# A two-layer hybrid decoder trunk: weight pairs in pieces of 512 columns, retention loads moved ahead, and a norm written over its input

## The chip, the cores and the metric

The kernel runs on one core of a Trainium2 chip. The metric is the device time of one execution in microseconds (us). The engines are named as the profile names them: PE (TensorE, matmul) and PEld (its weight loads), DVE (VectorE), ACT (ScalarE), POOL (GpSimd) and SP (SyncE). POOL and SP only issue DMAs here, apart from a few small copies on POOL.

## What is computed

The reference is one inference step of a two-layer trunk with d_model 1024, on 256 prompt positions and 8 sequences of 8 new positions, 320 columns together. Cut to what matters:

```python
for l in range(2):
    x = x + 0.5 * swiglu_ffn(rmsnorm(x, ffn1_norm[l]), ffn1_w_gu[l], ffn1_w_down[l])
    h = rmsnorm(x, mix_norm[l])
    q, k, v, g_ret, u, z, xbc, dt, gates = split(h @ w_in[l])
    y_ret = retention_branch(q, k, v, g_ret, state_ret[l])   # 4 heads, decay masks, gated norm
    y_s5  = s5_branch(u, state_s5[l])                        # 64 groups, complex diagonal scan
    y_ssd = ssd_branch(z, xbc, dt, state_ssm[l], state_conv[l])
    x = x + (sum of sigmoid(gate_i) * y_i) @ w_out[l]
    x = x + 0.5 * swiglu_ffn(rmsnorm(x, ffn2_norm[l]), ffn2_w_gu[l], ffn2_w_down[l])
y = rmsnorm(x, final_norm)
```

Outputs are y and the new states of the three branches.

## The kernel before, in words

Activations lie transposed: a tile `t` of 128 channels by 320 columns, eight of them for d_model. They come from one pool of 53 buffers (`NT`).

**Weights.** All matrices are float32 in memory. `stream` (L267) yields blocks of 128x128 in the order of use. It loads a chunk of 1024 columns (`CH`, eight blocks) with a DMA on SP's queue into one of three raw buffers (`wraw`), and turns it into a float32r pair: ACT copies it to `whi` (L280), DVE subtracts that from the raw chunk to make `wlo` (L281). There are two buffers each of `whi` and `wlo`. `proj` (L287) multiplies each block with three matmuls: high by high (L294), high by low (L295), low by high (L296), 24 matmuls a chunk, 554 chunks in all. `split` (L299) makes the same kind of pair of an activation: ACT L304, DVE L305.

**Order.** The program is built with a tile framework. Each engine's instructions are put in one fixed order when the kernel is built, by a priority that follows the order of the source, and by when a buffer of their pool is free. An instruction written inside `high_priority(offset=n)` counts as n instructions earlier; the load and the two copies of a chunk have n = 120 (`AHEAD`), and evacuations of some projections have 600 (`SOON`). On the chip an engine runs its list in order, each instruction waiting for its semaphores.

**Stages of a layer.** The first feed-forward net (in layer 0 the tables of the S5 branch are built beside it, L1178), then the mixer, then the second net. In the mixer, `norm` (L372) makes h: for each of eight tiles DVE computes h = X * gain * r into a new tile (L377) and `split` makes the pair. Until that is ready, the first projections (`ssd_dt` L429, `s5_u` L1194, `conv` L502) use pairs of the unnormalised X. X is read from DRAM again near the layer's end (L1427).

`weave` (L381) runs a list of main units, mostly projections, and advances side generators evenly beside it: SSD groups (L588), S5 blocks (L1209), and in the last two weaves of the mixer (L1397, L1398) the four retention heads (`ret_head`, L864), two a weave one after the other. A head has twelve steps. In its first it issues, on POOL's queue, two loads of its state (L870) and two table loads (L871): its decay mask `mk` (`tab(2 + hd)`) and the decay table `qd` (`tab(6)`, the same for all heads). `tab` (L206) takes a tile `t` and issues a DMA (L208). After two empty steps come the scores, multiplied by the mask (L882 to L884), and the decayed queries (L886); the pair of the keys (`stack`, L568: ACT L573, DVE L574) spread to the array's rows (L583); the outputs; the state update and its stores (L931, L940); then the loads of two gate rows `sd` (L943, `fetch` L1319), the norm over the head (`rstd_of`, L330: DVE L338 to L347, PE L335 and L350), and the gating (L953, L954). `ret_qk` (L793) makes queries and keys; DVE evacuates it at L808. `s5_block` loads an S5 state (L1226) that DVE reads at L1257.

Of the kernel before, what the change touches and what calls it, by code (L numbers as in the profile page):

```python
# [9 lines left out]
F32 = mybir.dt.float32  # L10
F32R = mybir.dt.float32r
I32 = mybir.dt.int32
AF = mybir.ActivationFunctionType
ALU = mybir.AluOpType
# [19 lines left out]
CH = 1024  # L34
# [14 lines left out]
S5P = ((0,), (1, 2), (3, 4), (5, 6), (7,))  # L49
AHEAD = 120  # L50
# [102 lines left out]
    return t.rearrange(f"p ({' '.join(names)}) -> p {' '.join(names)}", **dict(zip(names, shape)))  # L153


class Trunk:
    def __init__(self, tc, ap, depth, es):
        self.tc, self.nc, self.ap, self.depth = tc, tc.nc, ap, depth
        self.uid = 0
        P = lambda n, b, **kw: es.enter_context(tc.tile_pool(name=n, bufs=b, **kw))  # L160
        self.cp = P("consts", 1)
        self.wr = P("wraw", 3)
        self.wh = P("whi", 2)
        self.wl = P("wlo", 2)
        self.tp = P("t", NT)
        self.pA = P("a", NA)
        self.pB = P("b", 4)
        self.pS = P("s", 7)
        self.pC = P("c", 4)
        self.sm = P("sm", 1)  # L170
        self.pp = P("pp", 4, space=PSUM)
        self.pb = P("pb", 4, space=PSUM)
        self.dr = P("dr", 1, space=DRAM)
# [93 lines left out]
    def stream(self, name, l, width=128):  # L267
        nc = self.nc
        src = self.ap[name][l]
        n = src.shape[1]  # L270

        def gen():
            for c in range(0, n, CH):
                w = min(CH, n - c)
                raw = self.s("wraw", [128, CH], pool=self.wr)
                hi = self.s("whi", [128, CH], F32R, pool=self.wh)
                lo = self.s("wlo", [128, CH], F32R, pool=self.wl)
                with self.tc.high_priority(offset=AHEAD):
                    nc.sync.dma_start(out=raw[:, :w], in_=src[:, c:c + w])
                    nc.scalar.activation(hi[:, :w], raw[:, :w], AF.Copy)  # L280
                    nc.vector.tensor_tensor(lo[:, :w], raw[:, :w], hi[:, :w].bitcast(F32), op=ALU.subtract)  # L281
                for b in range(0, w, width):
                    yield hi[:, b:b + width], lo[:, b:b + width]

        return gen()

# [9 lines left out]
            nc.tensor.matmul(p[:, :T], wl, xh, start=False, stop=k == n - 1)  # L296
        return p

    def split(self, src, hi=None):  # L299

        nc = self.nc
        hi = self.t(F32R)
        lo = self.t(F32R)
        nc.scalar.activation(hi, src, AF.Copy)  # L304
        nc.vector.tensor_tensor(lo, src, hi.bitcast(F32), op=ALU.subtract)  # L305
        return hi, lo
# [65 lines left out]
    def norm(self, l, name, r):  # L372
        nc = self.nc
        hs = []
        for k in range(KD):
            h = self.t()
            nc.vector.scalar_tensor_tensor(h, self.X[k], self.col(l, name, k), r, op0=ALU.mult, op1=ALU.mult)  # L377
            hs.append(self.split(h))
        return hs

# [409 lines left out]
    def ret_tabs(self):  # L790
        self.rot = self.tab(0), self.tab(1)

    def ret_qk(self, l, h, rot):  # L793

        nc = self.nc
        sts = {}

        def unit(nme, hd):
            if nme not in sts:
                sts[nme] = self.stream(f"w_{nme}", l)  # L800
            cos, sin = self.rot
            p = self.proj(sts[nme], h())
            sw = self.t()
            o = self.t()
            with self.soon():
                nc.scalar.activation(sw[0:64], p[64:128, :T], AF.Copy)
                nc.scalar.activation(sw[64:128], p[0:64, :T], AF.Copy)
                nc.vector.tensor_tensor(o, p[:, :T], cos, op=ALU.mult)  # L808
            nc.vector.tensor_tensor(sw, sw, sin, op=ALU.mult)
            nc.vector.tensor_tensor(o, o, sw, op=ALU.add)  # L810
            rot[nme, hd] = o

        return [lambda n=n, hd=hd: unit(n, hd) for n in "qk" for hd in range(RH)]
# [50 lines left out]
    def ret_head(self, l, hd, rot, v, vs, sd, out):  # L864
        nc, C, ap = self.nc, self.C, self.ap
# [2 lines left out]
        s0 = [self.A(4, 256) for _ in range(2)]  # L868
        for i in range(2):
            nc.gpsimd.dma_start(out=s0[i], in_=ap["ret_in"][l][:, hd, 4 * i:4 * i + 4])  # L870
        mk, qd = self.tab(2 + hd), self.tab(6)  # L871
        yield
        yield
        q, k = rot["q", hd], rot["k", hd]
        vv, VS = v[hd // 2], vs[hd // 2]
        c8 = float(np.exp(LS * np.log1p(-np.exp2(-5.0 - hd))))
# [34 lines left out]
        for e in range(2):  # L911
            vc = slice(hd % 2 * 256 + e * 128, hd % 2 * 256 + e * 128 + 128)
            po = self.ps()
            nc.tensor.matmul(po[:, 0:256], vv[:, 0, vc], sc[:, 0:256], start=True, stop=False)
            nc.tensor.matmul(po[:, 128:256], vv[:, 1, vc], sc[:, 256:384], start=False, stop=True)
            nc.tensor.matmul(po[:, 256:320], vv[:, 2, vc], sc[:, 384:], start=True, stop=False)
            for hf in range(2):
                nc.tensor.matmul(po[:, 256 + 32 * hf:288 + 32 * hf], ys[hf][:, e * 128:e * 128 + 128], C["pick"],
                                 start=False, stop=hf == 1)
            o = self.t()  # L920
            S.activation(o, po[:, :T], AF.Copy)
            os.append(o)
            yield

        vh = slice(hd % 2 * 256, hd % 2 * 256 + 256)
        pp = self.ps()
# [13 lines left out]
                nc.gpsimd.dma_start(out=ap["ret_s"][l][:, hd, 4 * (b2 // 2):4 * (b2 // 2) + 4], in_=s0[b2 // 2])  # L940
                yield

        sgs = [self.fetch(sd[:, 2 * hd + e]) for e in range(2)]  # L943
        pm = self.ps()
        for e in range(2):
            nc.tensor.matmul(pm[:, :T], self.ones[256], os[e], start=e == 0, stop=e == 1)
# [3 lines left out]
        r = self.rstd(os, 256)  # L950
# [377 lines left out]
    def layer(self, l):  # L1328
        nc, ap = self.nc, self.ap
# [8 lines left out]
        hs, r = self.scaled(l, "mix_norm")  # L1338
# [3 lines left out]
        h = lambda: H[0]  # L1342
# [18 lines left out]
        s5 = lambda *bs: [(self.s5_block(l, Q, ud, yd, b), self.S5_STEPS) for b in bs]  # L1361
        zu = lambda g: self.ssd_gate(l, h, g, xg[g][2:], S["z"], yg[g])
# [3 lines left out]
        rot, v, vs, heads = {}, [], [], {}  # L1366
# [3 lines left out]
        sd = self.dr.tile([128, KD, T], F32, name=self.nm("sd"))  # L1370
# [6 lines left out]
        rg = self.ret_gate(l, h, S["g"], sd)  # L1377
        take = lambda n: [free.pop(0) for _ in range(n)]
# [4 lines left out]
        x, o = xu(3), ou(1)  # L1383
        self.weave(take(W4) + x[:2] + zu(1) + blend(x[2:], take(W5)) + take(W6) + o[:4] + [self.ret_tabs] + o[4:], ssd(2), s5(*S5P[0]))
        self.weave(take(W7) + qk[:2] + zu(2) + qk[2:5] + take(W8) + blend(qk[5:], ou(2)), ssd(3), s5(*S5P[1]))
        o = ou(3)
        self.weave(vu[0] + zu(3) + [vr] + vu[1] + o[:2] + [vr] + o[2:], s5(*S5P[2]))
        yret = []
        ret = [(self.ret_head(l, hd, rot, v, vs, sd, yret), self.RET_STEPS) for hd in range(RH)]

        def gate2(m):
            gt = self.gate(S["t2"], h())
            V.scalar_tensor_tensor(merged[m], gt, 1.0, merged[m], op0=ALU.add, op1=ALU.mult)

        g2 = [lambda m=m: gate2(m) for m in range(KD)]
        n = len(free)
        self.weave(rg[:4] + g2[:4] + take(n // 2), ret[:2], s5(*S5P[3]))  # L1397
        self.weave(rg[4:] + g2[4:] + take(len(free)), ret[2:], s5(*S5P[4]))  # L1398
        so = self.stream("ret_w_o", l)
        ys5 = []  # L1400
# [183 lines left out]
```

## Time and profile before

| what | value |
|---|---|
| median of 3 runs | 2372.28 us (2371.87 to 2375.01) |
| the profiled execution's own time | 2377.88 us |
| its span, first to last instruction | 2376.1 us |
| instructions | 41534 |
| HBM traffic | 455.63 MB, mean 192 GB/s |

The span is what one execution shows between its first and its last instruction; the few microseconds around it make the execution's time. Busy time of PE is modelled, since its matmuls overlap: a PE that is shown busy may still run below its peak. An idle time is put down to the instruction that released the waiting one.

### The profile page before, as it was taken

The page shows a single profiled execution, that of the slowest core. Times are in us where ns is not written, and L with a number is a line of the kernel's source. Part 1 is how long each engine was busy: PE and PEld are TensorE (multiplying, and loading weights), DVE is VectorE, ACT ScalarE, POOL GpSimd, SP SyncE. Part 2 cuts the span into 40 slices and gives each one's busy share as a digit, 9 for nine tenths or more (in the row PEclk, how much of TensorE's full clock was granted, in tenths as well). Part 3 has the DMA queues.
Part 4 walks back from the last instruction along what each step waited for, and adds up shares of the span by engine and source line. Part 5 has one row for each costly group of instructions (what it writes and reads, how often), then busy time and mean ns, then how long its engine had stood idle before and what let it go on. Part 6 is the DMA issues. An engine that isn't in the chain of part 4 may idle for free.

```text
span 2376.1 us, 41534 instructions
## 1 busy us (share of the span) xinstructions
PE 2294.7 (97%) x15798; PEld 2177.9 (92%) x15798; DVE 1754.0 (74%) x3398; ACT 1231.0 (52%) x2261; POOL 439.5 (18%) x858
## 2 busy tenths in 40 slices
PE   7999999999999999999999999999999999999998
PEld 7999989988898889999999999899888887999998
DVE  7989788798776556767876687888887665666554
ACT  4444477676454444444443445876574544544332
POOL 0111242221223230001000013432211232200000
PEclk9999999999999999999999999999999999999999
DMA  5767656756666565455556665766756674755553
GB/s 172 229 209 223 209 173 225 242 189 206 225 200 218 188 204 169 150 164 177 179 173 192 180 210 167 245 196 212 232 161 212 212 257 140 226 150 146 149 150 110
DMA packets 130856, 455.63 MB, mean 192 GB/s; under 512 B 19744, under 2 KB 23552, under 8 KB 130656
## 3 DMA queue, kind: packets, MB, share of 16 engines
q1 hardware_dynamic: 82080, 293.11, 40.7%
q0 software_dynamic: 48576, 159.86, 19.9%
q8 instruction: 124, 2.03, 0.3%
q14 instruction: 76, 0.62, 0.1%
HBM read 381.31 MB, written 72.89 MB: 191 GB/s over the span
## 4 chain that ended last, share of the span: by engine, by line
PE 78%; ACT 6%; DVE 6%; issue 5%; DMA 2%; POOL 2%; SPq 0%; DVEq 0%; POOLq 0%; ACTq 0%
PE pp L294 22%; PE pp L296 22%; PE pp L295 22%; DVE wlo L281 2%; ACT whi L280 2%; DMA t<-in_tabs 2%; PE pb L1238 1%; ACT B L671 1%; PE pb L350 1%; PE pb L711 1%; PE pb L718 1%; PE pb L687 1%; PE pp L836 1%; PE pp L837 1%; PE pp L838 0%
## 5 line engine op out<-in xcount | busy, mean ns | idle before, releaser
L294 PE MATMUL pp<-t,whi 128*128 128x320 f32 x4304 | 1344.2, 313 | 30.6 <-ACT t L365 12.3
L296 PE MATMUL pp<-t,wlo 128*128 128x320 f32 x4304 | 1339.5, 312 | 11.3 <-DVE wlo L281 11.1
L295 PE MATMUL pp<-t,whi 128*128 128x320 f32 x4304 | 1339.4, 312 | 0.4 <-DVE t L366 0.4
L280 ACT ACTIVATE whi<-wraw 128x1024 fp32r<-128x1024 f32 x554 | 586.2, 1059 | 779.1 <-issue 388.7
L281 DVE TENSOR_TENSOR wlo<-wraw,whi 128x1024 fp32r<-128x1024 f32 x554 | 676.7, 1222 | 265.5 <-ACT whi L280 261.9
L294 PEld LDWEIGHTS pp<-t,whi 128*128 128x128 f32 x4304 | 811.0, 189 | 49.1 <-ACT t L365 12.3
L296 PEld LDWEIGHTS pp<-t,wlo 128*128 128x128 f32 x4304 | 811.7, 189 | 25.4 <-DVE wlo L281 18.0
L295 PEld LDWEIGHTS pp<-t,whi 128*128 128x128 f32 x4304 | 812.3, 189 | 8.0 <-issue 2.6
L304 ACT ACTIVATE t<-t 128x320 fp32r<-128x320 f32 x184 | 84.3, 463 | 61.8 <-DVE t L1421 28.7
L305 DVE TENSOR_TENSOR t<-t,t 128x320 fp32r<-128x320 f32 x184 | 88.4, 486 | 18.1 <-ACT t L304 16.9
L526 DVE SCALAR_TENSOR_TENSOR acc<-xpad,cols,acc 128x344 f32<-128x344 f32 x144 | 80.0, 571 | 4.3 <-ACT acc L523 3.6
L405 DVE TENSOR_TENSOR t<-pp,t 128x320 f32<-128x320 f32 x88 | 42.7, 486 | 45.0 <-PE pp L296 39.0
L411 DVE TENSOR_TENSOR t<-t,pp 128x320 f32<-128x320 f32 x88 | 42.6, 484 | 38.6 <-PE pp L296 37.7
L671 ACT ACTIVATE B<-C,tk 128x128 f32<-128x128 f32 x192 | 63.0, 392 | 0.1
L325 ACT ACTIVATE t<-t 128x320 f32<-128x320 f32 x104 | 47.2, 460 | 25.7 <-DVE t L416 12.2
L416 DVE SCALAR_TENSOR_TENSOR t<-pp,t 128x320 f32<-128x320 f32 x64 | 31.2, 488 | 35.1 <-PE pp L296 35.0
L406 ACT ACTIVATE t<-t 128x320 f32<-128x320 f32 x88 | 40.4, 459 | 22.1 <-DVE t L405 22.0
L519 POOL COPY cso<-xpad 128x3 f32<-128x3 f32 x48 | 29.1, 607 | 104.9 <-ACT xpad L514 79.0
L1148 POOL DMA_DIRECT2D kd<-t x64 | 32.6, 516 | 78.5 <-issue 73.4
L407 DVE TENSOR_TENSOR t<-t,t 128x320 f32<-128x320 f32 x88 | 42.7, 485 | 4.5 <-ACT t L406 4.5
L1166 POOL DMA_DIRECT2D pk<-A x16 | 8.8, 552 | 188.4 <-DVE A L1164 188.4
L709 DVE TENSOR_TENSOR A<-A,dec 128x512 f32<-128x512 f32 x64 | 42.3, 685 | 1.3 <-PE pb L699 1.3
(368 smaller groups left out, 2508.8 us busy)
## 6 DMA issues: line engine op xcount, KB each, us to landing
wraw<-in_w_gu SPq DMA_DIRECT2D x176, 512.0 KB, 3.5
wraw<-in_w_down SPq DMA_DIRECT2D x88, 512.0 KB, 3.6
wraw<-in_w_xbc SPq DMA_DIRECT2D x48, 512.0 KB, 4.3
wraw<-in_w_gate SPq DMA_DIRECT2D x48, 512.0 KB, 4.6
A<-in_ssm_in POOLq DMA_DIRECT2D x32, 512.0 KB, 6.0
out_ssm_s<-A POOLq DMA_DIRECT2D x32, 512.0 KB, 5.1
wraw<-in_w_z SPq DMA_DIRECT2D x32, 512.0 KB, 4.8
wraw<-in_ssd_w_o SPq DMA_DIRECT2D x32, 512.0 KB, 3.7
```

The lines of the kernel that those rows point to most:

```text
L280: nc.scalar.activation(hi[:, :w], raw[:, :w], AF.Copy)
L281: nc.vector.tensor_tensor(lo[:, :w], raw[:, :w], hi[:, :w].bitcast(F32), op=ALU.subtract)
L294: nc.tensor.matmul(p[:, :T], wh, xh, start=k == 0, stop=False)
L295: nc.tensor.matmul(p[:, :T], wh, xl, start=False, stop=False)
L296: nc.tensor.matmul(p[:, :T], wl, xh, start=False, stop=k == n - 1)
L304: nc.scalar.activation(hi, src, AF.Copy)
L305: nc.vector.tensor_tensor(lo, src, hi.bitcast(F32), op=ALU.subtract)
L325: self.nc.scalar.activation(q, x, AF.Square)
L405: V.tensor_tensor(hid[i], p[:, :T], r, op=ALU.mult)
L407: V.tensor_tensor(hid[i], hid[i], r, op=ALU.mult)
L526: nc.vector.scalar_tensor_tensor(acc[:, :n], xp[:, r:r + n], self.col(l, "conv_w", 4 * i + r), acc[:, :n], op0=ALU.mult, op1=ALU.add)
L671: S.activation(lm[:, e, o:o + 128], bc[:, i0:i0 + 128], AF.Relu, scale=-1.0, bias=tk[:, b, c:c + 1])
```

## The change

It does four things. Weight chunks are still loaded in 1024 columns to three raw buffers, but the pairs are made in pieces of 512 columns (`CW`), with four buffers each of `whi` and `wlo` in place of two, each of half the size. `norm` writes h over X instead of into a new tile. A unit `ret_masks` loads the masks of heads 0 and 1 and the decay table in the last weave before retention, and those of heads 2 and 3 at the end of the first retention weave; `ret_head` no longer loads them. The two gate rows of a head are fetched before its state update instead of after it. (An argument of `split` that nothing used is dropped.)

```diff
+CW = 512
...
-        self.wh = P("whi", 2)
-        self.wl = P("wlo", 2)
+        self.wh = P("whi", 4)
+        self.wl = P("wlo", 4)
...
                 raw = self.s("wraw", [128, CH], pool=self.wr)
-                hi = self.s("whi", [128, CH], F32R, pool=self.wh)
-                lo = self.s("wlo", [128, CH], F32R, pool=self.wl)
                 with self.tc.high_priority(offset=AHEAD):
                     nc.sync.dma_start(out=raw[:, :w], in_=src[:, c:c + w])
-                    nc.scalar.activation(hi[:, :w], raw[:, :w], AF.Copy)
-                    nc.vector.tensor_tensor(lo[:, :w], raw[:, :w], hi[:, :w].bitcast(F32), op=ALU.subtract)
-                for b in range(0, w, width):
-                    yield hi[:, b:b + width], lo[:, b:b + width]
+                for o in range(0, w, CW):
+                    m = min(CW, w - o)
+                    hi = self.s("whi", [128, CW], F32R, pool=self.wh)
+                    lo = self.s("wlo", [128, CW], F32R, pool=self.wl)
+                    with self.tc.high_priority(offset=AHEAD):
+                        nc.scalar.activation(hi[:, :m], raw[:, o:o + m], AF.Copy)
+                        nc.vector.tensor_tensor(lo[:, :m], raw[:, o:o + m], hi[:, :m].bitcast(F32), op=ALU.subtract)
+                    for b in range(0, m, width):
+                        yield hi[:, b:b + width], lo[:, b:b + width]
...
         for k in range(KD):
-            h = self.t()
-            nc.vector.scalar_tensor_tensor(h, self.X[k], self.col(l, name, k), r, op0=ALU.mult, op1=ALU.mult)
+            h = self.X[k]
+            nc.vector.scalar_tensor_tensor(h, h, self.col(l, name, k), r, op0=ALU.mult, op1=ALU.mult)
             hs.append(self.split(h))
...
+    def ret_masks(self, *heads):
+
+        def unit():
+            if 0 in heads:
+                self.qd, self.mks = self.tab(6), {}
+            for hd in heads:
+                self.mks[hd] = self.tab(2 + hd)
+        return [unit]
...
-        mk, qd = self.tab(2 + hd), self.tab(6)
-        yield
-        yield
+        yield
+        yield
+        mk, qd = self.mks[hd], self.qd
...
             os.append(o)
             yield
+        sgs = [self.fetch(sd[:, 2 * hd + e]) for e in range(2)]
...
-        sgs = [self.fetch(sd[:, 2 * hd + e]) for e in range(2)]
         pm = self.ps()
...
-        self.weave(vu[0] + zu(3) + [vr] + vu[1] + o[:2] + [vr] + o[2:], s5(*S5P[2]))
+        self.weave(vu[0] + zu(3) + [vr] + vu[1] + o[:2] + [vr] + o[2:4] + self.ret_masks(0, 1) + o[4:], s5(*S5P[2]))
...
-        self.weave(rg[:4] + g2[:4] + take(n // 2), ret[:2], s5(*S5P[3]))
+        self.weave(rg[:4] + g2[:4] + take(n // 2) + self.ret_masks(2, 3), ret[:2], s5(*S5P[3]))
```

## Rows read from the trace of the kernel before

**Rows 1.** The page's part 1: busy us (share of the span) xinstructions.

```profile
PE 2294.7 (97%) x15798; PEld 2177.9 (92%) x15798; DVE 1754.0 (74%) x3398; ACT 1231.0 (52%) x2261; POOL 439.5 (18%) x858
```

**Rows 2.** Stretches of 25 us: busy time of each engine, PEclk, DMA share, GB/s.

```profile
50.00:75.00 25.00, 24.78 (x169) 24.51 (x168) 24.66 (x63) 14.61 (x28) 2.69 (x5) 1.00 0.59 183
...
1725.00:1750.00 25.00, 24.42 (x176) 23.65 (x175) 23.42 (x47) 22.25 (x53) 0.00 (x0) 1.00 0.45 141
...
2150.00:2175.00 25.00, 25.00 (x173) 25.00 (x172) 15.18 (x22) 9.93 (x14) 0.00 (x0) 1.00 0.51 148
```

**Rows 3.** Waits of PE: us in total, times, longest us.

```profile
PE pp L296 <- DVE wlo L281: 11.1, 16, 1.9
PE pb L583 <- DVE S L574: 9.3, 8, 2.0
PE pb L350 <- DVE rs L347: 8.5, 7, 2.3
...
PE pp L294 <- DVE t L808: 5.9, 2, 3.0
PE pp L294 <- ACT whi L280: 5.5, 9, 1.3
```

**Rows 4.** Waits of PE's weight loads.

```profile
PEld pp L296 <- DVE wlo L281: 18.0, 20, 2.2
...
PEld pp L294 <- ACT whi L280: 8.3, 11, 1.6
```

**Rows 5.** Timeline of an undisturbed chunk: start us, us, instruction, idle before it.

```profile
2151.17 1.06 ACT L280 ACTIVATE whi<-wraw 128x1024 fp32r<-128x1024 f32 x1 [2.10 <-issue]
...
2152.26 1.23 DVE L281 TENSOR_TENSOR wlo<-wraw,whi 128x1024 fp32r<-128x1024 f32 x1 [0.51 <-ACT whi L280]
```

**Rows 6.** Groups by line and shape: busy us, mean ns, idle before.

```profile
L281 DVE TENSOR_TENSOR wlo<-wraw,whi 128x1024 fp32r<-128x1024 f32 x554 | 676.7, 1222 | 265.5 <-ACT whi L280 261.9 <-PE pp L296 1.4
L280 ACT ACTIVATE whi<-wraw 128x1024 fp32r<-128x1024 f32 x554 | 586.2, 1059 | 779.1 <-issue 388.7 <-PE pp L295 352.1 <-PE pp L840 17.7
...
L304 ACT ACTIVATE t<-t 128x320 fp32r<-128x320 f32 x184 | 84.3, 463 | 61.8 <-DVE t L1421 28.7 <-DVE t L377 16.5 <-DVE t L411 10.1
...
L709 DVE TENSOR_TENSOR A<-A,dec 128x512 f32<-128x512 f32 x64 | 42.3, 685 | 1.3 <-PE pb L699 1.3
```

**Rows 7.** Timeline of DVE in a full stretch.

```profile
537.83 1.22 DVE L281 TENSOR_TENSOR wlo<-wraw,whi 128x1024 fp32r<-128x1024 f32 x1
538.96 0.68 DVE L712 TENSOR_TENSOR A<-A,pb 128x512 f32<-128x512 f32 x1
539.56 0.54 DVE L692 SCALAR_TENSOR_TENSOR t<-t,cols,pb 128x320 f32<-128x320 f32 x1
```

**Rows 8.** Waits of POOL.

```profile
POOL A L870 <- PE pb L1286: 12.1, 2, 6.1
```

**Rows 9.** Waits of DVE for DMAs: us in total, times, longest us.

```profile
DVE f L1257 <- DMA t<-in_s_in: 9.3, 7, 2.1
...
DVE pad L886 <- DMA t<-in_tabs: 8.4, 3, 4.3
DVE t L953 <- DMA t<-sd: 7.9, 6, 2.6
...
DVE S L882 <- DMA t<-in_tabs: 5.9, 4, 2.1
```

**Rows 10.** Group of POOL's table loads.

```profile
L208 POOL DMA_DIRECT2D t<-in_tabs x22 | 12.1, 553 | 0.0
```

**Rows 11.** Waits of ACT.

```profile
ACT t L304 <- DVE t L377: 16.5, 12, 2.7
```

**Rows 12.** The span and the mean granted clock of TensorE.

```profile
core 0: 2376.1 us, clock 0.989
```

More of the change, by code (lines that the diff above doesn't have):

```diff
@@ L297, in proj, with split @@
         return p
-    def split(self, src, hi=None):
+    def split(self, src):
         nc = self.nc
```

## Prediction

> **What bounds the kernel now.** I read the page's busy shares first: TensorE (PE) is busy in 97% of the span, VectorE (DVE) in 74%, ScalarE (ACT) in 52% [rows 1]. That share is modelled, so I went on to the table of 25 us stretches. Where nothing disturbs it, PE starts 173 matmuls in 25 us, 145 ns each; a chunk of eight weight blocks (24 matmuls) then takes 3.47 us and half a chunk 1.73 us. In the stretches at 50 and 1725 us DVE is busy over 23 of 25 us, and twelve of the 95 whole stretches are like this (these two are the first and the last) [rows 2]. So PE sets the time, and it can only get shorter by what PE loses: its waits, and the slower clock after them. The lists of waits say to whom it loses.
>
> PE waits 11.1 us for the low half of a weight pair (`wlo`, L281) and 5.5 us for the high half (`whi`, L280); 9.3 us for L574 and 8.5 us for L347, two DVE results in the retention and norm chains; 5.9 us for L808, a projection that DVE evacuates late [rows 3]. A matmul's end is modelled, so these are the short reading; the weight loads, which precede the matmuls, wait 18.0 us and 8.3 us for the two halves of the pair [rows 4].
>
> **Part 1: pieces of 512 columns, four buffers.** In undisturbed stretches ACT begins a chunk's `whi` at 2151.17, when a buffer comes free, and DVE ends its `wlo` at 2152.26 + 1.23 = 2153.49 [rows 5]: 2.3 us of the 3.47 us that PE takes for the other buffer. About 1.1 us is left, and every delay of ACT or DVE beyond that stops PE. With pieces the bytes held are the same, but a piece is free after half a chunk and is used again three pieces later, after 3 x 1.73 = 5.2 us. Its two copies take less: ACT needs 1059 ns for 1024 columns and 463 ns for 320, which puts 512 on 626 ns; a DVE operation on two 128x512 operands took 685 ns [rows 6]. 5.2 - 1.3 leaves 3.9 us, more than the longest single wait for a piece (1.9 us on PE). The waits bound the gain from above, 26.3 us by weight loads and 16.6 us by matmuls; from below it is nothing, because where DVE is full a piece is late however early its buffer is free. I take 15 us, near the matmuls' reading. PE's waits for pieces double in number, but those already met show no gap in the 145 ns spacing: nothing.
>
> What it costs: by durations a chunk costs DVE 2 x 685 - 1222 = 148 ns more and ACT 2 x 626 - 1059 = 193 ns more, 82 and 107 us over 554 chunks. But starts lie closer than durations: `wlo` to the next operation 1.13 us, a 512-column operation to the next 0.60 us [rows 7], so two pieces cost DVE 0.07 us more a chunk, 39 us in all. Both engines idle hundreds of us and cover that; where DVE is full it isn't covered. Twelve stretches with seven chunks each: 84 x 0.07 = 6 us by starts, 84 x 0.148 = 12 us by durations. I take 5 us, since part of DVE's work in those stretches is not due at once. ACT has room even there: 22.25 us in the stretch at 1725 [rows 2], plus 7 x 0.19 is 23.6 of 25.
> The Trainium skill (VectorE: DVE Perf Modes, section "The DRAIN you can't avoid") says that the next DVE operation does not start until the pipe has emptied. By that rule the term would be 12 us. The trace disagrees for these operations: L712 starts at 538.96, before `wlo` ends at 539.05 [rows 7].
> The raw buffers stay three, and SP reloads one when its last `wlo` is done. The second piece waits for the same half chunk as before and is copied in 1.3 us where 2.3 us was needed, so reloads start no later: nothing.
>
> **Part 2: the retention loads.** Each of the four heads of a layer issues its mask and the same decay table on POOL's queue, behind its two state loads, which wait for a buffer that PE still reads (12.1 us in two places) [rows 8]. DVE then stands at the head's first multiplications: 8.4 + 5.9 us for the tables, 7.9 us for the gate rows (`t<-sd`) [rows 9], and the conversions behind them stand too, since an engine works in order. The new units issue the masks before those state loads and the table once, three loads fewer a layer at 0.55 us of POOL [rows 10]; the gate rows go ahead of the head's state stores. What they are moved past: on POOL the S5 loads of the same stage move back by three issues, 1.7 us, a layer. I cost that at nothing, since those loads are issued several steps before use; without that cover it is up to 3.4 us over both layers. Four or five work tiles are held longer, and a late tile would show as a wait of a DMA or a gate. SP's queue isn't touched. For PE this is worth between 0 and 9.3 + 8.5 = 17.8 us, its waits just behind [rows 3]; not all of those follow a late load, so I take 9 us.
>
> **Part 3: the norm over X.** The same instruction, written in place; no new tile is needed. Before, ACT waits 16.5 us in 12 places for L377 [rows 11]: each next L377 stands behind the split of the one before, though its inputs are there, which looks like a pool without a free tile. Then ACT's next `whi` stands behind those splits. Worth 0 to 5.5 us (all of PE's wait for `whi`) [rows 3]; I take 2 us.
>
> **The clock.** The mean granted clock is 0.989 [rows 12]; 1.1% of the span is 26 us of full-clock time. Part of it is the kernel's end; the rest I read as the price of PE's longer stalls. Fewer of them give back between nothing and some 10 us, under half of it; I take 4 us.
>
> **Sum:** -15 + 5 - 9 - 2 - 4 = -25 us. The profiled execution took 2377.88 us, 5.6 us above the median of the three runs, 2372.28 us. It would become 2353; against the median I forecast **2347 us**.
>
> **Rivals.**
> *The next wait takes the place.* DVE's in-order list has more behind the masks: L1257 waits 9.3 us for the S5 state load [rows 9], L808 is late because DVE is full, and a mask issued on a POOL queue that stands is no earlier. Then pieces give 8 us, masks 3 us, norm and clock nothing, DVE costs 3 us: 2364 us. For it: all these rows. Against it: most waits for `wlo` are shorter than the new 3.9 us of room.
> *Slower: DVE becomes the bound.* Its place is the twelve full stretches. If starts spread to full durations there (+12 us) and PE's waits turn into waits for evacuations such as L808, nothing is gained: 2372 + 12 = 2384 us. It decides once DVE's busy time in such a stretch reaches 25 us: 24.66 + 7 x 0.148 is 25.7 in the worst one [rows 2], while by starts it is 25.1. That one is mostly table building, which can slip; so I give it little.
> The rule of the Trainium skill's page VectorE: DVE Perf Modes cited above would make this rival true; the trace speaks against it [rows 7].
> *More than the sum.* DVE sits 261.9 us behind ACT's `whi` [rows 6]; if that blocking in order is what makes other DVE work late, it shrinks too. Terms near their upper ends, -24, -16, -5, -10, cost 3: -52, 2320 us.
> That the change doesn't do what it says is inside the first rival: the order on each engine is settled when the kernel is built, and a mask can land in it no earlier.
>
> **How the numbers follow.** Forecast 0.62 (its own range 2332 to 2362), next wait 0.18, slower 0.12, more 0.08. The range 2324 to 2376 takes in the forecast's bounds, the first rival and the rest down to most of the fourth; it leaves out the slower case. Under 0.2% (4.7 us) a measurement can't tell a change here: faster by over that is 0.62 + 0.08 + 0.10 of the first rival, 0.80; within it 0.08; slower 0.12.
>
> **What would show it.** Right: waits of PE and its weight loads for `wlo` and `whi` well under half; DVE's waits for the tables and the gate rows near zero; `wlo` x1108 near 685 ns; ACT no longer waiting for L377 in such a row; mean clock above 0.989; DVE busy up by 40 to 80 us, PE's start-to-start spacing unchanged. Wrong: PE's waits moved to L808, L680 or L1257's followers at the same sum, DVE full in the same stretches with PE below its 24 us there, or the masks issued behind the same standing POOL instruction as before.

## The result: 0.7% faster, and the profile after

The changed kernel takes 2358.86 us (median of 4 runs, 2356.11 to 2360.85) beside 2372.91 us (2371.87 to 2375.01) of the kernel before on the same chip: a ratio of 0.9931, 95% interval 0.9915 to 0.9947. The forecast was 2347 us in a range of 2324 to 2376. Direction and range held; the gain is 14 us by the medians, 16 by the ratio, where 25 were summed.

The whole-kernel views of the profile after: the page's part 1 answers to [rows 1], the span to [rows 12].

```profile
PE 2286.4 (97%) x15798; PEld 2173.3 (92%) x15798; DVE 1809.4 (77%) x3952; ACT 1350.6 (57%) x2823; POOL 428.9 (18%) x852
```

```profile
core 0: 2359.0 us, clock 0.990
```

DVE is busy 55 us more and ACT 120 us more. PE's busy time, which holds the matmuls at half clock too, fell by 8 us, and its mean clock rose by 0.001. The groups by line, which answer to [rows 6], give the two copies of a piece:

```profile
L287 DVE TENSOR_TENSOR wlo<-wraw,whi 128x512 fp32r<-128x512 f32 x1108 | 757.8, 687 | 319.5 <-ACT whi L286 302.3 <-PE pp L302 2.3
L286 ACT ACTIVATE whi<-wraw 128x512 fp32r<-128x512 f32 x1108 | 695.5, 631 | 812.3 <-PE pp L301 665.5 <-issue 37.4 <-PE pp L855 17.2
```

687 and 631 ns, where 685 and 626 were forecast. Now the lists of waits of the kernel after (us in total, times, longest us), which answer to [rows 3, 4, 9, 11] (L280 and L281 are L286 and L287 now, L574 is L580, L1257 is L1272):

```profile
...
PE pb L341 <- DVE t L333: 6.7, 9, 1.7
PE pb L589 <- DVE S L580: 4.6, 3, 3.5
PE pb L641 <- DVE S L580: 4.2, 6, 3.1
PE pb L693 <- DVE A L718: 3.7, 2, 2.3
PE pp L300 <- DVE t L823: 3.6, 4, 1.5
PE pp L302 <- DVE wlo L287: 3.3, 6, 1.8
...
PE pp L300 <- ACT whi L286: 3.0, 3, 1.9
...
PEld pp L300 <- ACT whi L286: 8.7, 11, 2.1
...
PEld pp L302 <- DVE wlo L287: 5.9, 9, 2.0
...
DVE f L1272 <- DMA t<-in_s_in: 21.2, 10, 5.2
...
DVE pad L901 <- DMA t<-in_tabs: 0.4, 1, 0.4
```

Most waits that the change was aimed at are gone or small: PE waits 3.3 us for `wlo` (11.1 before) and its weight loads 5.9 us (18.0), DVE waits 0.4 us for the tables (14.3 before) and no longer for the gate rows (7.9 before), and ACT's wait for L377 (now L383) has left its list. Two are not small. The wait for `whi` fell only from 5.5 to 3.0 us on PE, and on the weight loads it is 8.7 us (8.3 before), where well under half was forecast. PE's wait at L583 for L574 was 9.3 us; for the same instruction, L580 now, it waits 4.6 us there and 4.2 us at L641 (0.5 before, at L635), with single waits of 3.5 and 3.1. What has grown is DVE's wait for the S5 state load, 9.3 to 21.2 us, with one of 5.2. That one is worth following: a part of the missing gain went there. DVE's timeline at the place (start, us, instruction, idle before it):

```profile
703.16 0.21 DVE L899 TENSOR_TENSOR S<-pb,t 128x64 f32<-128x64 f32 x1
708.61 0.23 DVE L1272 TENSOR_TENSOR f<-t,se 128x64 f32<-128x64 f32 x1 [5.24 <-DMA t<-in_s_in]
708.75 0.22 DVE L1273 TENSOR_TENSOR f<-t,se 128x64 f32<-128x64 f32 x1
709.00 0.23 DVE L1274 TENSOR_TENSOR f<-f,f 128x64 f32<-128x64 f32 x1
709.26 0.29 DVE L580 TENSOR_TENSOR S<-S,S 64x128 fp32r<-64x128 f32 x1
```

L580, 0.29 us long, makes the keys of the first retention head ready for TensorE. It stands behind three operations of the S5 block, the first of which waits for a load. PE waits 3.5 us for it, and then runs at half clock, as the table of stretches shows (stretch, its length, busy time of PE, PEld, DVE, ACT, POOL; then PEclk, DMA share, GB/s):

```profile
700.90:705.80 4.90, 4.90 (x36) 4.85 (x36) 1.92 (x5) 2.78 (x7) 1.47 (x3) 1.00 0.98 331
705.80:709.60 3.80, 0.34 (x3) 0.08 (x1) 0.89 (x5) 0.95 (x2) 0.55 (x1) 0.87 0.47 185
709.60:717.20 7.60, 7.51 (x45) 5.76 (x46) 1.50 (x3) 2.01 (x6) 0.00 (x0) 0.50 0.24 69
717.20:720.70 3.50, 3.50 (x20) 3.50 (x20) 2.69 (x7) 2.52 (x8) 0.00 (x0) 0.77 0.00 0
```

In these four stretches PE starts about a hundred matmuls in 19.8 us; the last experiment shows the same work in 11.9.

### The profile page after: what moved, and what is told of

It is laid out like the page before. It is cut to its first block, busy times and chain, and to the rows that moved or that the text cites. A ratio compares the mean times of both kernels' runs of the same rounds, so it can differ in the third digit from the quotient of the medians.

```text
span 2359.0 us, 43431 instructions
## 1 busy us (share of the span) xinstructions
PE 2286.4 (97%) x15798; PEld 2173.3 (92%) x15798; DVE 1809.4 (77%) x3952; ACT 1350.6 (57%) x2823; POOL 428.9 (18%) x852
## 3 DMA queue, kind: packets, MB, share of 16 engines
q0 software_dynamic: 48288, 158.88, 19.9%
## 4 chain that ended last, share of the span: by engine, by line
PE 56%; DVE 2%; ACT 2%; issue 1%; DMA 1%; POOL 0%; DVEq 0%; ACTq 0%; POOLq 0%
PE pp L300 17%; PE pp L302 16%; PE pp L301 16%; DVE wlo L287 1%; ACT whi L286 1%; PE pb L341 0%; PE pb L356 0%; DMA wraw<-in_w_gate 0%; PE pp L853 0%; PE pb L1253 0%; PE pp L851 0%; PE pp L852 0%; PE pb L1301 0%; PE pb L724 0%; PE pb L693 0%
## 5 line engine op out<-in xcount | busy, mean ns | idle before, releaser
L286 ACT ACTIVATE whi<-wraw 128x512 fp32r<-128x512 f32 x1108 | 695.5, 631 | 812.3 <-PE pp L301 665.5
L287 DVE TENSOR_TENSOR wlo<-wraw,whi 128x512 fp32r<-128x512 f32 x1108 | 757.8, 687 | 319.5 <-ACT whi L286 302.3
L300 PEld LDWEIGHTS pp<-t,whi 128*128 128x128 f32 x4304 | 809.7, 189 | 44.4 <-ACT t L371 12.3
L310 ACT ACTIVATE t<-t 128x320 fp32r<-128x320 f32 x184 | 84.1, 467 | 10.9 <-DVE t L417 5.6
L718 DVE TENSOR_TENSOR A<-A,pb 128x512 f32<-128x512 f32 x64 | 41.8, 679 | 0.4 <-PE pb L717 0.4
L525 POOL COPY cso<-xpad 128x3 f32<-128x3 f32 x48 | 21.0, 437 | 112.8 <-ACT xpad L520 89.1
```

What stands on the lines that cost most here:

```text
L286: nc.scalar.activation(hi[:, :m], raw[:, o:o + m], AF.Copy)
L287: nc.vector.tensor_tensor(lo[:, :m], raw[:, o:o + m], hi[:, :m].bitcast(F32), op=ALU.subtract)
L300: nc.tensor.matmul(p[:, :T], wh, xh, start=k == 0, stop=False)
```

## The experiments

Each text of expectation was written before its run and says in its own words what its theories are. Times are compared by their ratio to the kernel before on the same chip, since its median differs between chips (2373 to 2380 us). "So many us" is the ratio's distance from 1 times 2372.

**The parts alone.** e1 is the kernel before with the pieces alone, e2 with the norm over X alone, e3 with the masks, the table and the gate rows ahead of use alone. Each edit is that part of the diff shown above; the core of each:

```diff
+                for o in range(0, w, CW):
...
-            h = self.t()
+            h = self.X[k]
...
-        mk, qd = self.tab(2 + hd), self.tab(6)
+        mk, qd = self.mks[hd], self.qd
```

> The kernel before with the pieces of 512 columns and four buffers alone. Theory A (the pieces bring nearly all of it): the same -14 us as the whole change, 2356 to 2362 us, with waits of PE and its weight loads for whi and wlo down from 26 us (weight loads) to under 16. Theory B (each part brings its share): -8 us, 2362 to 2367 us. Theory C (DVE's and ACT's added work eats what the pieces free): within 3 us of before.

> The kernel before with the norm written over X alone. Theories A and C: within 3 us of before, since few waits of PE follow the norm. Theory B: -2 to -6 us; ACT's wait for the norm's product (16.5 us before) falls under 5 us, and PE's wait at 302 to 313 us of layer 0 goes.

> The kernel before with the masks and the gate rows loaded ahead, alone. Theory A (the next wait takes the place: DVE then stands at L1257 for the S5 state load): within 4 us of before, DVE's waits for the tables gone, its wait for the S5 state load up from 9.3 us to 15 or more. Theory B: -5 to -9 us, the wait for the S5 state load about as before.

Measured: e1 0.9991 (0.9975 to 1.0007), nothing that can be told from no change; e2 0.9941 (0.9921 to 0.9962), 14 us; e3 0.9914 (0.9898 to 0.9930), 20 us. So by the time alone theory C holds for the pieces (its reason, the added work, is tested in e5), and the other two parts gained more than any of the theories gave them.

e1 did to its own waits what was forecast, and TensorE then waited for others. PE's waits in e1:

```profile
...
PE pb L589 <- DVE S L580: 9.9, 7, 1.9
PE pb L356 <- DVE rs L353: 8.3, 10, 2.4
PE pp L300 <- ACT t L310: 6.7, 5, 1.8
PE pb L341 <- DVE t L333: 6.3, 9, 1.7
...
PE pp L302 <- DVE wlo L287: 3.3, 6, 1.8
```

The wait for `wlo` fell by 7.8 us and that for `whi` by 4.0 (5.5 to 1.5), but the waits for ACT's split (L310; L304 before) rose from 3.1 to 6.7 and those for L333 (L327 before) from 2.8 to 6.3. Matmul 2000 starts 5.2 us sooner than before, matmul 2500 0.7 us later: what the pieces gain in one stretch, the next gives back.

e2 shows why the norm was worth more than its bound. Here are PE's waits in layer 0 between 225 and 386 us in the kernel before, the first four rows of that list:

```profile
PE pb L687 <- DVE B L680: 3.1, 3, 2.1
PE pp L294 <- DVE t L436: 2.8, 1, 2.8
PE pp L294 <- ACT whi L280: 1.3, 1, 1.3
PE pp L296 <- DVE wlo L281: 1.0, 2, 0.7
```

and TensorE's clock (PEclk, third number from the end) around the stall of 2.8 us:

```profile
285.20:288.00 2.80, 0.04 (x1) 0.07 (x1) 1.81 (x3) 0.96 (x1) 0.00 (x0) 1.00 0.34 139
288.00:291.40 3.40, 3.40 (x14) 3.40 (x15) 2.62 (x7) 0.94 (x2) 1.63 (x5) 0.55 0.70 202
```

In the same matmuls of e2 (225 to 377.5 us) none of these four is left in the list. What heads it is this:

```profile
PE pp L294 <- ACT t L304: 2.8, 1, 2.8
PE pp L294 <- DVE xpad L518: 0.7, 1, 0.7
```

In this stretch ACT waits 9.6 us for L377 before and not at all in e2, and the waits of four other lines go with it: 8 us less from matmul 1500 to 2500, and 7 us less again in layer 1.

In e3 (DVE's waits) the table and gate rows are gone, and the state load waits no longer than before:

```profile
DVE f L1267 <- DMA t<-in_s_in: 8.8, 7, 2.1
```

**The two that gain, together (e4), and the pieces' instructions without their buffers (e5).** e4 is the whole change with the pieces undone. e5 is e4 with each chunk's two copies made in two halves of 512 columns, in the same two buffers of 1024.

```diff
-                    nc.scalar.activation(hi[:, :w], raw[:, :w], AF.Copy)
-                    nc.vector.tensor_tensor(lo[:, :w], raw[:, :w], hi[:, :w].bitcast(F32), op=ALU.subtract)
+                    for o in range(0, w, 512):
+                        nc.scalar.activation(hi[:, o:o + 512], raw[:, o:o + 512], AF.Copy)
+                        nc.vector.tensor_tensor(lo[:, o:o + 512], raw[:, o:o + 512], hi[:, o:o + 512].bitcast(F32), op=ALU.subtract)
```

> The changed kernel with the pieces undone (chunks of 1024 columns, two buffers); norm in place and loads ahead stay. Theory A: within 4 us of the kernel before. Theory B: -6 us, 2364 to 2369 us. Theory C: at or below the whole change's time, 2359 us or less.

> The kernel of e4 (no pieces; norm in place, loads ahead) with each chunk's two copies made in two halves of 512 columns, into the same two buffers of 1024: as many ACT and DVE instructions as with the pieces, but buffers come free by chunks as before. Theory W (the work of twice as many instructions is what the pieces cost): about as slow as the whole change, 2354 to 2362 us. Theory O (the order: with four small buffers the copies stand earlier in the lists of ACT and DVE, and evacuations stand behind copies that wait for PE or for a raw load): within 4 us of e4, 2343 to 2351 us.

Measured: e4 0.9870 (0.9851 to 0.9890), 31 us; e5 0.9870 (0.9837 to 0.9902). So two parts of the change are worth 31 us, the whole 16: the pieces, on top of the others, cost some 14 us. And the number of their instructions is not the reason (theory O's forecast for e5 held, theory W's failed): e5 has as many copies as the whole change and costs nothing that can be told, although DVE is busy 1788.9 us in it and 1753.3 in e4. Nor is it the wait for the S5 state load by itself, which is as long in e5 as in the whole change (21.2, longest 5.2):

```profile
DVE f L1268 <- DMA t<-in_s_in: 21.0, 8, 5.3
```

**Lead and the state load (e6, e7, e8).** AHEAD says how many instructions early a chunk's load and copies are placed in the built lists. e6 is the whole change with AHEAD 60 for 120; e8 is e4 with AHEAD 130. e7 is the whole change with the S5 block's state load issued ahead of the block's other loads:

```diff
+        st0 = self.tv(2, NG, NB)
+        nc.gpsimd.dma_start(out=st0, in_=ap["s5_in"][l][:, :, gs])
         od, cp, rt = self.A(1152), self.A(1024), self.A(1024)
...
-        st0 = self.tv(2, NG, NB)
-        nc.gpsimd.dma_start(out=st0, in_=ap["s5_in"][l][:, :, gs])
```

> The whole change with AHEAD at 60 in place of 120, so that loads and copies are put in the lists less far ahead. Theory O: 4 to 12 us faster than the whole change, 2347 to 2355 us, with fewer waits of PE behind DVE results. Theory W: within 3 us of the whole change or slower, since less lead helps nothing.

> The whole change with the S5 state load of a block issued first instead of last among the block's loads. Theory N (in retention DVE's next wait, for the S5 state, took the place of the masks'): DVE's wait at the first use of the S5 state falls from 21 us to under 9, PE's wait for the keys' pair (3.5 us at 709 us) goes, 4 to 9 us faster than the whole change. Theory O or W alone: within 3 us of the whole change.

> A control: the kernel of e4 with AHEAD at 130 in place of 120, which only nudges the order. If the parts measured so far are worth what they seem: within 3 us of e4, 2344 to 2350 us. If orders differ by chance as much as the parts do: 5 us or more from e4, either way.

Measured: e6 0.9985 (0.9971 to 0.9999), 13 us slower than the whole change; e7 0.9957 (0.9941 to 0.9973), 6 us slower; e8 0.9826 (0.9799 to 0.9853), 10 us faster than e4. Three misses of what I thought likeliest. Less lead is worse, not better (theory W allowed for that, but had failed in e5): in e6 PE waits 14.4 us for `whi`. The state load's wait did fall in e7, from 21.2 to 15.2 us, but not where it hurts: at the first retention head of layer 0 it is still 4.63 us. The load is issued there at 700.72 us, 3.1 us before DVE asks for it, and takes 7.75 us to land. And e8, meant as a control that moves next to nothing, moved the time by 10 us, a size that its text gives to orders that differ by chance.

**Is it lead, the buffers, or the order that was built? (e9, e10, e11).** e9 is the whole change with AHEAD 130. In e10 (AHEAD 120) both pieces of a chunk are copied in one place:

```diff
+                ps = []
                 for o in range(0, w, CW):
...
-                    for b in range(0, m, width):
+                    ps.append((m, hi, lo))
+                for m, hi, lo in ps:
+                    for b in range(0, m, width):
```

e11 is e4 with AHEAD 160.

> The whole change with AHEAD 130 for 120 (the lead, in built instructions, with which a weight chunk's load and copies are placed ahead of its matmuls); e8 was the same step for the version without pieces: 2336.6 beside a kernel before of 2376.5, 0.9826. Theory L (the pieces' price of 14 us is lead: the second piece's copies are built after the first piece's matmuls, so they land later in the lists of ACT and DVE): 10 more give the second piece part of its lead back, 2342 to 2352 us, 0.986 to 0.990, nearer to e8 than the whole change is to e4. Theory G (the price belongs to the finer buffers themselves: each copy waits in order for its own piece to come free, and what stands behind it waits too): the price stays 14 us, 2350 us, 0.989. Theory C (the built order moves the time by some 10 us either way, whatever the edit): no tie to e8; any value from 0.984 to 0.997, and PE's waits in other places.

> The whole change, but the copies of both pieces of a chunk are built together at the chunk's start, so that the second piece has the lead that the whole chunk had before; four buffers of 512 columns as in the whole change, AHEAD 120. Theory L: the price of the pieces goes, 2345 to 2351 us, 0.987 to 0.990, as in e4 (0.987) and e5 (0.987). Theory G: the buffers and their order of use are those of the whole change, so it stays at 0.993 (2356 to 2362 us), with ACT still standing some 665 us at whi for PE. Theory C: no tie to either; 0.984 to 0.997.

> e4 (the change without pieces) with AHEAD 160; 120 gave 0.987, 130 gave 0.9826. Theory L in its broad form (more lead is better, since evacuations and state work stand behind copies that come late): at least as fast as with 130, 0.979 to 0.983, 2326 to 2337 us. Theory C: 130 was a good draw among orders, so 160 falls back to somewhere between 0.983 and 0.992, 2337 to 2358 us. Too much lead (copies stand in ACT's and DVE's lists for buffers that aren't free, ahead of work that is due): slower than e4, over 0.988, with ACT's and DVE's waits at whi and wlo up.

Measured: e9 0.9880 (0.9857 to 0.9903); e10 0.9915 (0.9892 to 0.9939); e11 0.9812 (0.9787 to 0.9836), 2332.60 us beside 2379.99, the lowest of all and 45 us below the kernel before by the ratio. The number of e9 fits theories L and G alike; e10 missed L's range and is near G's; e11 fits L's. Lead is a lever of its own: with pieces 60, 120, 130 give 0.9985, 0.9931, 0.9880; without them 120, 130, 160 give 0.9870, 0.9826, 0.9812. With the pieces the three intervals lie apart; without them those of 120 and 130 touch and those of 130 and 160 overlap. A pure draw of orders (theory C) would hardly line up so, though these runs do not rule it out. And at either lead the pieces cost the same, 14 us at 120 and 13 at 130, so lead isn't what they lack; e10, with the lead given back, still stands 11 us above e4. PE's wait for `wlo` in e4, e8 and e11, in this order:

```profile
PE pp L296 <- DVE wlo L281: 9.3, 13, 1.9
```

```profile
PE pp L296 <- DVE wlo L281: 5.7, 14, 0.7
```

```profile
PE pp L296 <- DVE wlo L281: 2.4, 6, 0.7
```

More lead does to this wait, in two whole buffers, what four half buffers did (3.3): this speaks for the copies having been late by their place in ACT's and DVE's lists more than by the buffer.

To find the 14 us I read from each trace when the n-th matmul starts. Two stretches, the first retention head of each layer, tell the versions apart (us that 100 matmuls take; worked out from the starts of the matmul records, each rounded to 0.1 us):

```
kernel                         4650 to 4750   12550 to 12650
before                              12.8          12.3
e1 pieces alone                     13.6          12.7
e2 norm alone                       12.3          12.6
e3 loads alone                      12.1          12.2
e4, e5, e8, e11 (no pieces)     12.1 to 12.2  12.2 to 12.3
whole change                        19.8          12.2
e6 whole, lead 60                   17.1          18.4
e7 whole, state load first          18.9          17.4
e9 whole, lead 130                  20.0          19.5
e10 whole, copies together          19.4          20.3
```

Only where pieces and loads come together does a stretch take 17 to 20 us. The difference between e9 and e8 is 16.7 us of span, and these two stretches hold 15.1 of it. In other versions the two don't add up so well: against e4 they hold 7.8 of 11.8 us in the whole change, 12 of 16.8 in e7, and in e10 some 15 where the spans differ by 7.5. The first is the place shown above. In the versions without pieces the built list has the head's conversion ahead of the state operations; DVE in e4:

```profile
704.61 0.21 DVE L893 TENSOR_TENSOR S<-pb,t 128x64 f32<-128x64 f32 x1
704.86 0.29 DVE L574 TENSOR_TENSOR S<-S,S 64x128 fp32r<-64x128 f32 x1
707.83 0.23 DVE L1267 TENSOR_TENSOR f<-t,se 128x64 f32<-128x64 f32 x1 [2.68 <-DMA t<-in_s_in]
```

DVE waits for the load there too, but nobody waits for DVE.

The traces show this order at both heads: in each of the six versions without pieces and in the kernel before, the conversion stands ahead of the state operations; in each version with pieces up to here, e1 too, it stands behind the first of them, the one that waits for the load. So the pieces turn the order, but in e1 it costs little, because the load is nearly in. The load's issue on POOL in e1 and DVE's two operations, then the issue in the whole change:

```profile
708.77 0.72 POOL L1232 DMA_DIRECT2D t<-in_s_in  x1
714.50 0.23 DVE L1263 TENSOR_TENSOR f<-t,se 128x64 f32<-128x64 f32 x1 [0.48 <-DMA t<-in_s_in]
714.90 0.29 DVE L580 TENSOR_TENSOR S<-S,S 64x128 fp32r<-64x128 f32 x1
```

```profile
702.76 0.71 POOL L1241 DMA_DIRECT2D t<-in_s_in  x1 [1.67 <-DMA A<-pk]
```

In e1 DVE asks for the load 5.25 us after its issue (at 714.02), in the whole change 0.61 us after it (at 703.37). Counted in matmuls, the load is issued 13 later than in e1 and asked for 17 sooner. That is why pieces and loads cost together what neither costs alone at this place. Two runs point to the four small buffers as what turns the order: e5 and e10 make the same copies, both halves in one place; e5, with two whole buffers, keeps the conversion ahead, and e10, with four, has it behind.

**One instruction moved (e12).** The whole change, with the conversion bound to come first in that one block:

```diff
-        nc.vector.tensor_tensor(hl[:NS], rows, hl[NS:].bitcast(F32), op=ALU.subtract)
+        self.stk = nc.vector.tensor_tensor(hl[:NS], rows, hl[NS:].bitcast(F32), op=ALU.subtract)
...
-        step(st0[:, 0], st0[:, 1], 0, so[:, :, :, 1])
+        with self.tc.issue_after(self.stk.ins) if (l, blk) == (0, S5P[3][0]) else nullcontext():
+            step(st0[:, 0], st0[:, 1], 0, so[:, :, :, 1])
```

In the built program one DVE instruction stands three places earlier; the lists of the other engines are the same.

> The whole change with one DVE instruction three places earlier in the built list and nothing else moved on any engine: in layer 0's first retention head, the subtraction at L580 (before, L574) is built ahead of the three state operations L1272 to L1274 of the S5 block, as it stands in the versions without pieces (e4, e5). In the whole change those wait 5.2 us for the state load there, L580 behind them, PE 3.5 us for L580, and half clock follows. Theory P (the pieces' price on top of the loads is mostly the place that the build gives this instruction, not the pieces themselves): PE's wait of 3.5 us and the half clock after it go, 6 to 8 us less than the whole change: 2351 to 2353 us, 0.989 to 0.991. Theory G (the finer buffers cost it): the place is only where the loss shows, and the same time is lost behind the next late operation: 0.993, 2356 to 2361 us.

Measured: the profiled execution took 2352.07 us, its span 2350.3 (2359.0 for the whole change). At the place, DVE in e12:

```profile
700.87 0.29 DVE L580 TENSOR_TENSOR S<-S,S 64x128 fp32r<-64x128 f32 x1 [0.55 <-ACT S L579]
705.03 0.23 DVE L1272 TENSOR_TENSOR f<-t,se 128x64 f32<-128x64 f32 x1 [3.87 <-DMA t<-in_s_in]
```

and the same work of TensorE as in the four stretches above, at full clock:

```profile
697.80:709.70 11.90, 11.90 (x102) 11.02 (x101) 6.00 (x18) 7.55 (x21) 2.08 (x4) 1.00 0.65 217
```

11.9 for 19.8 us: the price of this place is 7.9 us, as theory P had it, and in this trace it does not come back behind the next late operation: e12 is 3.0 us ahead of the whole change at matmul 4650, 11.0 at 4750, and 11.6 to 12.3 from 5000 to 10500. It comes back in the twin place, layer 1's first head, which the edit leaves alone: there the stretch takes 19.9 us in e12 and 12.2 in the profile of the whole change. The built order there is the same in both; it hangs on when the load arrives. PE's wait in e12 between 1845 and 1880 us:

```profile
PE pb L589 <- DVE S L580: 3.4, 1, 3.4
```

POOL issues that load at 1854.59 in e12, after waiting 2.19 us for another DMA, and without that wait in the profile of the whole change, where DVE then waits 1.77 us instead of 5.04 and PE not at all.

Over all executions the move is not shown to gain anything: 0.9923 (0.9899 to 0.9946), against 0.9931 (0.9915 to 0.9947) for the whole change. The six took 2352.07 us (the profiled one) and 2359.00 to 2363.18, beside 2372.28 to 2389.19 for the kernel before on that chip. The median, 2360.32 us, lies in theory G's range (2356 to 2361) and not in theory P's; by the ratio, P's 0.989 to 0.991 was missed, and the interval reaches both. So the trace speaks for P and the times do not. What the five without a trace lost, and where, stays open. Binding the twin place too was not run.

## Why the prediction was right, and which steps failed

*Bound and direction: right.* TensorE sets the time in both kernels (busy 97% of the span before and after; the matmuls of its largest group take 313 ns in both), and the gain came from its waits and the clock behind them. DVE did not become the bound. That the number held as well owes much to luck: three of its parts were off by more than the sum in the end was, in opposite directions, as follows.

*Part 1, "I take 15 us" less 5 for the copies: failed.* The waits for `wlo` went as forecast (on PE 11.1 to 3.3 us), those for `whi` only in part. But they were not worth their length: alone the pieces gave 2 us within an interval that holds nothing, since the waits for the split and L333 took the place. On top of the other parts they cost 14 us. The step that failed is "from below it is nothing": I let a part gain nothing but not lose, and looked for a loss only in DVE's busy time. Why the build lists them so was not traced, but what the pieces changed was the order in which the build lists DVE's instructions, and in that order an operation that TensorE waits for stands behind a load. Shown by traces: the place, its 7.9 us, and its absence once the instruction is moved. Also shown: the twin's 5 to 8 us in five traces. Not shown: that these two are all of the 14 us in every execution, nor that moving the one instruction shortens the kernel (e12 by its median does not). Where the rest of the 14 us goes stays open.

*"DVE costs 5 us": failed, on the safe side.* Twice the copies cost nothing that can be told (e5 against e4). In the whole change the operation after a `wlo` of 0.69 us starts 0.61 us after it (702.02 and 702.63). The Trainium skill (VectorE: DVE Perf Modes, section "The DRAIN you can't avoid") has the rule by which this term would be 12 us, but the section goes on that a next operation that is not held starts earlier. The prediction left that exception out. The early starts here and in [rows 7] fit it, so they are no evidence against the page, as the prediction has them.

*Part 2, "I take 9 us": undersized.* 20 us (17 to 24), with most of the interval above the upper end of 17.8. PE's wait for L574 fell from 9.3 to 0.8 us and for L347 from 8.5 to 3.4 in e3, 13.6 us in all, and the mean clock rose to 0.993, which the bound had left to another term. The cost of moving the S5 loads back on POOL, "I cost that at nothing", held by itself: 8.8 us of waits in e3 against 9.3. Beside the other parts it did not: 12.9 us in e4, 21.0 in e5 and 21.2 in the whole change, where an operation that PE needs stands behind one of these waits.

*Part 3, "worth 0 to 5.5 us, I take 2": undersized most.* 14 us. The mechanism was right, ACT standing for L377. The bound was wrong: it counted only PE's waits for `whi`, while the split's delay also reached L436, L680 and `wlo`, and half clock followed the longest of them.

*The clock, "I take 4 us":* as a term of its own it was a mistake. Its price belongs to each long stall: the stall of 3.5 us cost 7.9, and the mean clock of the whole change is 0.990 beside 0.989.

*The rivals.* "The next wait takes the place" is what happened to part 1, at the very line that it named: L1257's wait for the state load. It was paid by parts 2 and 3, which gave 31 us together where 11 were summed. So the sum came out 9 us off with three of its terms off by more than that, in both directions: the pieces with their copies by 24 us (a gain of 10 taken, a cost of 14 on top of the others), the loads by 11 and the norm by 12 the other way.

## What to carry to other kernels

Bound what a wait is worth not by that one line of the list of waits but by all waits within the reach of the late instruction, and add the half clock behind the longest. A change of the buffers, or of how early instructions are placed, can redraw the order in which an engine's instructions are built: look in the new list for an operation that the bounding engine needs and that now stands behind one that waits for a load, and try moving that one. Before adding buffers or cutting instructions up, try the lead: 40 instructions more of it, in one constant, took the version with the norm and the loads but without pieces from 0.9870 to 0.9812 (2332.60 us). What lead alone does to the kernel before was not run.

## What the runs showed of the hardware

Two stalls of TensorE cost more than twice their length. After 3.5 us of waiting for one instruction the granted clock was 0.50, the lower of its two levels (1.2 of 2.4 GHz), for 7.6 us, and the stretch took 19.8 us where it takes 11.9 without the stall. With the stall of 3.4 us in e12 layer 1's stretch took 19.9 us, and 12.2 in the whole change, which has no such stall there. After the 2.8 us stall of the kernel before it averaged 0.55 over the next 3.4 us. Two versions with the same built order at that place of layer 1 thus differ there by nearly 8 us, by how long DVE waits for a load on POOL's queue (5.04 and 1.77 us). That load's time from issue to landing ran from 2.4 to 9.2 us over its 16 issues in the whole change. And 554 further copies each on DVE and ACT, the columns as before, cost nothing that can be told (e4 and e5, both 0.9870).
